# A gated linear-recurrence mixer: its projections as seven block products per pair of matrices, its head outputs through DRAM, its output projection at the end

## The chip, the cores and the metric

The kernel runs on one core of a Trainium2 chip. The metric is the device time of a run in microseconds, as the median of several runs. Engines: TensorE (PE, matmuls, its weight loads as PEld), VectorE (DVE), ScalarE (ACT), GpSimd (POOL) and SyncE (SP, whose queue issues nearly all DMAs). Matmuls write to PSUM banks of 128 partitions by 512 fp32; data otherwise lies in SBUF, 128 partitions wide.

## The reference

One layer on x of 1024 tokens by 1024 channels, in fp32: a mixer, then an MLP, each with RMSNorm ahead and a residual add.

```python
h = rmsnorm(x, norm_mix)
q, f, i, g = split(h @ w_in, 4)              # w_in: 1024 x 4096; 8 heads of 128 channels
log_f = log(lb + (1 - lb) * sigmoid(f));  k = (1 - lb) * sigmoid(-f);  q = silu(q) * 128 ** -0.5
# per head, v = i:  S_t = diag(f_t) S_(t-1) + k_t v_t^T,   o_t = S_t^T q_t
o = o * rsqrt(mean(o * o) + eps) * out_norm * silu(g)        # mean over a head's 128 channels
x = x + o @ w_out
x = x + relu(rmsnorm(x, norm_mlp) @ w1) ** 2 @ w2            # hidden 4096
return rmsnorm(x, norm_final)
```

## The kernel before

Every fp32 product is three matmuls: each operand is split into a rounded part (hi, written by ACT) and the rest (lo, a subtraction on DVE), and split_mm (L171) issues hi·hi, hi·lo, lo·hi.

**Norm and transposes.** x (8 tiles of 128 tokens, xs) is scaled (L144) and turned by PE (L155), so that channels lie on partitions (hT, two halves of 512 tokens, 8 blocks kb of channels).

**Projections, head by head.** proj_qf (L279) makes q and f with channels on partitions: 2 projections × 2 halves × 8 kb × 3 = 96 matmuls of 128x512, tile qf. proj_vg (L323) makes v and g with tokens on partitions: 8 token blocks × 8 kb × 3 = 192 matmuls of 128x256, tile vg. Weights come in pieces of 128x1024 by load_raw (L103) and are split by ensure (L110; L119 on ACT, L120 on DVE), five pieces a head with the one of w_out.

**The scan** of a head is a list of units (scan_units, L350): small, middle, leaf, big(32) and big(64) are small matmuls (tile lv, L366, L399, L417, L447) that fill the decay matrix level by level, each followed by a chain on DVE that carries q, k and f to the next level (carry_q L254, carry_k L261, carry_f L267; prefixes_2 makes qe with two copies on ACT, L388 and L392, and L393 on DVE); kt turns k, kv makes the states S, o_unit the output o, whose squares ACT sums (L499); GpSimd makes the factor rs_z from them (L77 an add, L78 a power), z_unit scales z by it on ACT (L508), and zt turns z (L516). pump (L194) spreads the units over the projections: each three matmuls add 650 (330 for the narrow ones), and when a spacing (2000, or 1800 for the first heads and the last) is reached, the next unit is issued; None is an empty unit. So the program's text fixes PE's order, and every unit must find its chain done. DVE, ACT and POOL take their order from the program up to in_order.close(); behind it a scheduler sets it.

**Output projection.** proj_out (L526): for every head 16 groups of three matmuls of 128x512 (tile op), each added to xs by DVE (L536), one head behind the projections. zt stays in SBUF, split, until then.

**MLP.** It already works by seven block products per pair of blocks (products m1, m2 with banks X, Y, Z; sums of blocks of weights and activations; activations through DRAM, adB and adt). Between mixer and MLP x is normed and turned again (hm and hn, L655).

Of the kernel before, what the change touches and what calls it, by code (L numbers as in the profile page):

```python
# [47 lines left out]
def trunk(ctx: ExitStack, tc: tile.TileContext, x, gains, masks, gfin, w_in, w_out, w1, w2, out):  # L48
# [3 lines left out]
    rstack = ExitStack()  # L52
    res = rstack.enter_context(tc.tile_pool(name="res", bufs=1, side="right", reuse_waits="tile"))
# [49 lines left out]
    def load_raw():  # L103
        i = len(raws)
        if i < len(srcs):
            raw = pool.tile([P, D], F32, name=f"raw{i}", tag="raw", bufs=2)
            nc.sync.dma_start(raw, srcs[i])
            raws.append(raw)

    def ensure(n):  # L110

        while len(split) < min(n, len(srcs)):
            i = len(split)
            raw = raws[i]
            w = pool.tile([P, 2, D], F32R, name=f"w{i}", tag="w", bufs=5)
            step = D // 4 if i < 2 else D
            for c in range(0, D, step):
                o = slice(c, c + step)
                nc.scalar.activation(w[:, 0, o], raw[:, o], AF.Copy)  # L119
                nc.vector.tensor_tensor(w[:, 1, o], raw[:, o], w[:, 0, o].bitcast(F32), ALU.subtract)  # L120
# [897 lines left out]
```

## Time and profile before

| | |
|---|---|
| runs | 1214.08, 1218.25, 1215.22 us; median 1215.22 |
| profiled execution | 1218.23 us, of which the span in the profile 1216.4 us; mean granted clock 0.994 |
| busy in the span | PE 1193.6, DVE 755.9, ACT 516.5, POOL 43.0 us |
| a head in the middle (from one head's first projection to the next head's) | 67.29 us |

The profile shows one execution: a row of the timeline is the start, the duration, the engine, line, operation, output and inputs, shape, and in brackets the idle time ahead with what ended it. A group by line has total busy time, mean ns, and idle time ahead. A row of waits has the total, the count and the longest. Durations of matmuls overlap; their starts don't.

### The profile page before, as it was taken

The page shows a single profiled execution, that of the slowest core. Times are in us where ns is not written, and L with a number is a line of the kernel's source. Part 1 is how long each engine was busy: PE and PEld are TensorE (multiplying, and loading weights), DVE is VectorE, ACT ScalarE, POOL GpSimd, SP SyncE. Part 2 cuts the span into 40 slices and gives each one's busy share as a digit, 9 for nine tenths or more (in the row PEclk, how much of TensorE's full clock was granted, in tenths as well). Part 3 has the DMA queues.
Part 4 walks back from the last instruction along what each step waited for, and adds up shares of the span by engine and source line. Part 5 has one row for each costly group of instructions (what it writes and reads, how often), then busy time and mean ns, then how long its engine had stood idle before and what let it go on. Part 6 is the DMA issues. An engine that isn't in the chain of part 4 may idle for free.

```text
span 1216.4 us, 19005 instructions
## 1 busy us (share of the span) xinstructions
PE 1193.6 (98%) x7980; PEld 1016.7 (84%) x7980; DVE 755.9 (62%) x1071; ACT 516.5 (42%) x899; POOL 43.0 (4%) x78
## 2 busy tenths in 40 slices
PE   8999999999999999999999999999999999999997
PEld 8889889898989899887778888888887888888886
DVE  5475747475665745666865456545657874677663
ACT  6444433333332423335645445454453353233542
POOL 2100000000000000001000000000000000000011
PEclk9999999999999999999999999999999999999999
DMA  6111111111011111113042445224696663522431
GB/s 229 53 54 36 36 53 36 35 37 53 19 53 36 46 44 36 36 36 132 25 173 104 173 173 190 117 109 156 233 339 243 231 215 140 173 70 89 136 121 70
DMA packets 36806, 131.92 MB, mean 108 GB/s; under 512 B 4208, under 2 KB 4336, under 8 KB 36720
## 3 DMA queue, kind: packets, MB, share of 16 engines
q1 hardware_dynamic: 36000, 129.65, 29.8%
q8 instruction: 62, 1.02, 0.3%
q10 hardware_dynamic: 720, 1.07, 0.2%
q14 instruction: 24, 0.20, 0.0%
HBM read 92.95 MB, written 37.75 MB: 107 GB/s over the span
## 4 chain that ended last, share of the span: by engine, by line
PE 90%; DVE 4%; ACT 3%; issue 1%; POOL 1%; DMA 0%; POOLq 0%; DVEq 0%; ACTq 0%
PE vg L172 5%; PE m2X L174 5%; PE m2X L173 5%; PE qf L172 5%; PE m2X L172 5%; PE qf L174 5%; PE qf L173 5%; PE vg L173 5%; PE vg L174 5%; PE m1X L174 4%; PE m1X L172 4%; PE m1X L173 4%; PE m2Y L173 2%; PE m2Y L174 2%; PE m1Y L172 2%; PE m1Y L174 2%
## 5 line engine op out<-in xcount | busy, mean ns | idle before, releaser
L172 PE MATMUL vg<-w,hT 128*128 128x256 f32 x512 | 149.7, 292 | 0.0
L173 PE MATMUL vg<-w,hT 128*128 128x256 f32 x512 | 145.1, 283 | 0.0
L174 PE MATMUL vg<-w,hT 128*128 128x256 f32 x512 | 145.0, 283 | 0.0
L172 PE MATMUL qf<-hT,w 128*128 128x512 f32 x256 | 102.1, 399 | 0.0
L172 PEld LDWEIGHTS vg<-w,hT 128*128 128x128 f32 x512 | 98.2, 192 | 2.8
L174 PE MATMUL qf<-hT,w 128*128 128x512 f32 x256 | 100.2, 391 | 0.0
L173 PE MATMUL qf<-hT,w 128*128 128x512 f32 x256 | 100.0, 391 | 0.0
L173 PEld LDWEIGHTS vg<-w,hT 128*128 128x128 f32 x512 | 98.4, 192 | 0.4
L174 PEld LDWEIGHTS vg<-w,hT 128*128 128x128 f32 x512 | 98.4, 192 | 0.0
L823 ACT ACTIVATE a<-ai 128x1024 fp32r<-128x1024 f32 x56 | 58.9, 1052 | 66.4 <-PE m2X L173 20.5
L536 DVE TENSOR_TENSOR x<-x,op 128x512 f32<-128x512 f32 x120 | 78.3, 684 | 4.6 <-PE op L174 4.3
L824 DVE TENSOR_TENSOR a<-ai,a 128x1024 fp32r<-128x1024 f32 x56 | 68.3, 1220 | 16.2 <-ACT a L823 16.2
L120 DVE TENSOR_TENSOR w<-raw,w 128x1024 fp32r<-128x1024 f32 (+1 forms) x46 | 49.3, 1082 | 16.8 <-ACT w L119 16.6
L174 PEld LDWEIGHTS qf<-hT,w 128*128 128x128 f32 x256 | 48.2, 188 | 10.3
L172 PEld LDWEIGHTS qf<-hT,w 128*128 128x128 f32 x256 | 48.4, 189 | 9.5
L173 PEld LDWEIGHTS qf<-hT,w 128*128 128x128 f32 x256 | 48.3, 189 | 9.3
L172 PE MATMUL op<-w,zt 128*128 128x512 f32 x128 | 52.4, 410 | 1.4 <-DVE x L536 1.4
L706 ACT ACTIVATE e<-e 128x1024 f32<-128x1024 f32 x21 | 22.3, 1062 | 67.6 <-DVE e L858 67.6
L173 PE MATMUL op<-w,zt 128*128 128x512 f32 x128 | 50.6, 395 | 0.0
L174 PE MATMUL op<-w,zt 128*128 128x512 f32 x128 | 50.5, 395 | 0.0
L254 DVE TENSOR_TENSOR q<-q,f 128x512 f32<-128x512 f32 x56 | 38.6, 689 | 16.7 <-PE lv L447 14.5
L119 ACT ACTIVATE w<-raw 128x1024 fp32r<-128x1024 f32 (+1 forms) x46 | 42.8, 944 | 7.9 <-issue 5.1
(667 smaller groups left out, 2947.7 us busy)
## 6 DMA issues: line engine op xcount, KB each, us to landing
raw<-in_w_in SPq DMA_DIRECT2D x32, 512.0 KB, 3.7
ai<-adt SPq DMA_DIRECT2D x32, 512.0 KB, 4.5
adB<-e SPq DMA_DIRECT2D x24, 512.0 KB, 2.6
adt<-t SPq DMA_DIRECT2D x24, 512.0 KB, 4.9
ai<-adB SPq DMA_DIRECT2D x24, 512.0 KB, 4.5
x<-in_x SPq DMA_DIRECT2D x8, 512.0 KB, 7.3
raw<-in_w_out SPq DMA_DIRECT2D x8, 512.0 KB, 4.1
ua<-in_w SPq DMA_DIRECT2D x8, 512.0 KB, 6.0
```

Of the source, the lines that this page charges most:

```text
L119: nc.scalar.activation(w[:, 0, o], raw[:, o], AF.Copy)
L120: nc.vector.tensor_tensor(w[:, 1, o], raw[:, o], w[:, 0, o].bitcast(F32), ALU.subtract)
L172: nc.tensor.matmul(ps, lhi, rhi, start=start, stop=False, **more)
L173: nc.tensor.matmul(ps, lhi, rlo, start=False, stop=False, **more)
L174: nc.tensor.matmul(ps, llo, rhi, start=False, stop=stop, **more)
L254: nc.vector.tensor_tensor(qo, qo, te.to_broadcast([P, n, m]), ALU.mult)
L536: nc.vector.tensor_tensor(xs[tb][:, o], xs[tb][:, o], p_, ALU.add)
L706: nc.scalar.activation(t, t, AF.Relu, scale=sign)
L823: nc.scalar.activation(hi, x, AF.Copy)
L824: nc.vector.tensor_tensor(lo, x, hi.bitcast(F32), ALU.subtract)
```

## The change

q and f are one pair of projections, v and g another, each a product of a 2x2 block matrix (the pair's weights by halves of the input channels) with hn (by halves of channels and of tokens). For heads 1 to 7 each pair is made by seven block products of 4 kb × 3 = 12 matmuls of 128x512 (pair, L405), into three PSUM banks X, Z, Y whose partial results are taken out between the products; head 0's are plain (plain_pair, L379). Everything has channels on partitions, so v needs a unit of its own that turns it (vt, 8 transposes). The sums of blocks: of hn once (values R added by GpSimd, block_sums, split_sum), of weights per pair (four adds and seven splits of 128x512 on DVE, ensure). (1 − lb) of k is folded into q. z is scaled straight from PSUM, multiplied by the gate as it is turned, and stored to DRAM for heads 0 to 6 (z_d). At the mixer's end z and w_out are fetched in halves, split, and the output projection sums over seven heads in PSUM, then head 7, for one half of the columns, and over eight for the other; x, whose tiles were scaled in place, is loaded again (xr). The spacing is 1730. In the MLP some sums are made earlier, and the combinations of block 0 later.

```diff
+SPACING = 1730.0
-FILL = 2
+AHEAD = 6
...
+    def block_sums():
+        for k in range(2):
+            nc.vector.tensor_tensor(R[0, k], R[0, k], R[1, k], ALU.subtract)
+        for k in range(2):
+            nc.vector.tensor_tensor(R[1, k], R[1, 2 + k], R[1, k], ALU.subtract)
+        for k in range(2):
+            nc.vector.scalar_tensor_tensor(R[1, 2 + k], R[0, k], -1.0, R[1, 2 + k], op0=ALU.mult, op1=ALU.subtract)
+        for k in range(2):
+            nc.vector.scalar_tensor_tensor(R[0, 2 + k], R[1, 2 + k], -1.0, R[0, 2 + k], op0=ALU.mult, op1=ALU.subtract)
+    def split_sum(n):
+        half, k0 = SUMS[n]
+        for kb in range(4):
+            r = R[half, k0 + kb // 2][:, kb % 2]
+            if n == "t4":
+                t = hslot(1, kb, f"ht4{kb}")
+            else:
+                t = dslot(("t1", "t2", "t3").index(n) * 4 + kb, [P, 2, 512], f"h{n}{kb}", F32R)
+            hc[n, kb] = t
+            nc.scalar.activation(t[:, 0], r, AF.Copy)
+            nc.vector.tensor_tensor(t[:, 1], r, t[:, 0].bitcast(F32), ALU.subtract)
...
+    PLAIN = 2
+    ORDER = (("X", "a", "B11"), ("Z", "b", "B21"), ("X", "s2", "t2"), ("Y", "s1", "t1"),
+             ("X", "s3", "t3"), ("Y", "s4", "B22"), ("X", "d", "t4"))
...
+    def ensure(count):
+        while len(split) < min(count, len(jobs)):
             i = len(split)
+            n, m = jobs[i]
+            r = raws[n]
+            if m == "s1":
+                add(r["a"], r["a"], r["c"])
+                add(r["c"], r["c"], r["d"])
+            if m == "s2":
+                add(r["c"], r["a"], r["d"])
+            if m == "s4":
+                add(r["c"], r["c"], r["b"])
+            src = r[{"s1": "c", "s2": "c", "s4": "c", "s3": "a"}.get(m, m)]
+            w = mslot(4 + i % 8, [P, 2, 512], f"w{n}{m}", F32R)
+            step = P if i < 1 else 512
+            for c in range(0, 512, step):
                 o = slice(c, c + step)
-                nc.scalar.activation(w[:, 0, o], raw[:, o], AF.Copy)
-                nc.vector.tensor_tensor(w[:, 1, o], raw[:, o], w[:, 0, o].bitcast(F32), ALU.subtract)
+                nc.scalar.activation(w[:, 0, o], src[:, o], AF.Copy)
+                nc.vector.tensor_tensor(w[:, 1, o], src[:, o], w[:, 0, o].bitcast(F32), ALU.subtract)
             split[i] = w
+            if m == "d":
+                load_raw(n + 2)
...
+        def transposes_1(half):
+            def one(kb):
+                flat, g, t = transposed(0, half, kb, xs[4 * half:4 * half + 4])
+                nc.scalar.activation(t[:, 0], flat, AF.Copy, scale=g)
+                nc.vector.scalar_tensor_tensor(t[:, 1], flat, g, t[:, 0].bitcast(F32), op0=ALU.mult, op1=ALU.subtract)
+                if kb % 2 == 0:
+                    R[half, kb // 2] = value(half, kb // 2)
+                nc.gpsimd.tensor_tensor(R[half, kb // 2][:, kb % 2], t[:, 0].bitcast(F32), t[:, 1].bitcast(F32), ALU.add)
+            return [lambda kb=kb: one(kb) for kb in range(KB)]
...
+        def pair(h, tl, j):
+            n = 2 * h + j
+            bank = {}
+            for i, (b, m, src) in enumerate(ORDER):
+                first = b not in bank
+                if first:
+                    bank[b] = psum.tile([P, 512], F32, name=f"p{b}{n}", tag="d")
+                p_ = bank[b]
+                w = weight(n, m)
+                for kb in range(4):
+                    c = slice(kb * P, (kb + 1) * P)
+                    t = hc[src, kb]
+                    split_mm(p_, w[:, 0, c], w[:, 1, c], t[:, 0], t[:, 1], first and kb == 0, kb == 3,
+                             skip_group_check=True)
+                    if kb == 1:
+                        ensure(index[n, m] + AHEAD)
+                    pump(650.0)
+                if m in ("a", "s2", "s4", "b"):
+                    name = "q" if j == 0 else "vT"
+                    tiles(h, tl, name)
+                    half = int(m in ("s2", "s4"))
+                    dst = tl[name][:, HALF[half]]
+                    if m in ("a", "s2"):
+                        nc.scalar.activation(dst, p_, AF.Copy)
+                    else:
+                        add(dst, dst, p_)
+                        if j == 0 and half:
+                            q_part(h, tl, 0, tl["q"])
+                elif m == "s1":
+                    e = part(h, f"e{j}")
+                    nc.scalar.activation(e, p_, AF.Copy)
+                elif m == "s3":
+                    add(e, e, p_)
+                    (f_half, g_half)[j](h, tl, 1, e, -1.0)
+                else:
+                    (f_half, g_half)[j](h, tl, 0, p_, -1.0)
+                    if j == 0:
+                        f_bound(h, tl["f"])
...
+            def vt():
+                v = st["v"] = sp.tile([P, NC, P], F32, name=f"v{h}", tag="v")
+                for g in range(2):
+                    ps = psum.tile([P, 4, P], F32, name=f"vt{h}{g}", tag="s")
+                    for j in range(4):
+                        c = 4 * g + j
+                        nc.tensor.transpose(ps[:, j, :], tl["vT"][:, c * P:(c + 1) * P], ident)
+                    nc.scalar.activation(v[:, 4 * g:4 * g + 4, :], ps, AF.Copy)
+                free("vT")
...
+            def z_unit():
+                for c in range(NC):
+                    nc.scalar.activation(st["z"][:, c, :], st["o"][c // 4][:, c % 4, :], AF.Copy,
+                                         scale=st["r"][:, c:c + 1])
...
+            def zt():
+                z = tl["sg"]
+                for a in range(2):
+                    ps = psum.tile([P, 4, P], F32, name=f"zt{h}{a}", tag="s")
+                    for j in range(4):
+                        nc.tensor.transpose(ps[:, j, :], st["z"][:, 4 * a + j, :], ident)
+                    o = HALF[a]
+                    nc.vector.scalar_tensor_tensor(z[:, o], ps.rearrange("p a b -> p (a b)"), gz[:, h:h + 1], z[:, o],
+                                                   op0=ALU.mult, op1=ALU.mult)
+                    if h < NH - 1:
+                        nc.sync.dma_start(z_d[h][:, o], z[:, o])
+                free("sg")
...
-            return ([None] * (4 if h in (0, NH - 1) else 3) + [small, None, None] + [middle, None, leaf(16, 7)]
-                    + [big(32), big(64), kt, ("values", h), kv, o_unit, z_unit, ("out", h - 2), zt])
+            return ([None] * (6 if h == 0 else 3) + [small, None, None] + [middle, None, leaf(16, 7)]
+                    + [big(32), big(64), None, kt, ("values", h), vt, kv, None, o_unit, z_unit, None, zt])
...
+        heads = {0: {}}
+        tl = heads[0]
+        plain_pair(0, tl, 0, 0)
+        plain_pair(0, tl, 1, 0)
+        while hooks:
+            hook()
+        in_order.close()
+        block_sums()
+        for n in ("t1", "t3", "t2"):
+            split_sum(n)
+        AT = sp.tile([P, NC, P], F32, name="AT", tag="AT")
+        nc.gpsimd.memset(AT, 0.0)
+        plain_pair(0, tl, 0, 1)
+        prefixes(tl)
+        units.extend(scan_units(0, tl))
+        plain_pair(0, tl, 1, 1)
+        split_sum("t4")
+        complete.add(("values", 0))
+        for h in range(1, NH):
+            tl = heads[h] = {}
+            pair(h, tl, 0)
+            prefixes(tl)
+            units.extend(scan_units(h, tl))
+            if h == NH - 1:
+                spacing[0] = LAST_SPACING
+            pair(h, tl, 1)
+            complete.add(("values", h))
...
+        def split_value(t, src):
+            nc.scalar.activation(t[:, 0], src, AF.Copy)
+            nc.vector.tensor_tensor(t[:, 1], src, t[:, 0].bitcast(F32), ALU.subtract)
+        def fetch(what, half, lo, hi):
+            for h0 in range(lo, hi, 2):
+                raw = mslot(item_no[0] % 4, [P, 2, 512], f"i{what}{half}{h0}")
+                item_no[0] += 1
+                for i in range(min(2, hi - h0)):
+                    h = h0 + i
+                    src = z_d[h][:, HALF[half]] if what == "z" else w_out[h * P:(h + 1) * P, HALF[half]]
+                    nc.sync.dma_start(raw[:, i], src)
+                for i in range(min(2, hi - h0)):
+                    h = h0 + i
+                    t = (zh if what == "z" else wo)[half, h] = place(what, half, h)
+                    split_value(t, raw[:, i])
...
+        def proj_out(tbs, dh, hs, after=None):
+            o = HALF[dh]
+            for tb in tbs:
+                c = slice(tb % 4 * P, (tb % 4 + 1) * P)
+                p_ = psum.tile([P, 512], F32, name=f"op{dh}{tb}{hs[0]}", tag="d")
+                for i, h in enumerate(hs):
+                    z, w = zh[tb // 4, h], wo[dh, h]
+                    split_mm(p_, z[:, 0, c], z[:, 1, c], w[:, 0, o0], w[:, 1, o0], i == 0, i == len(hs) - 1)
+                    pump(650.0)
+                add(xs[tb][:, o], xs[tb][:, o], p_)
+                if after:
+                    after(tb)
...
+        fetch("z", 0, 0, last)
+        fetch("w", 0, 0, last)
+        for tb in range(NC):
+            load_x(tb)
+        proj_out(A, 0, range(last))
+        fetch("z", 1, 0, last)
+        fetch("w", 0, last, NH)
+        proj_out(B, 0, range(last))
+        fetch("w", 1, 0, 4)
+        drain_units()
+        for half in range(2):
+            t = zh[half, last] = place("z", half, last)
+            split_value(t, heads[last]["sg"][:, HALF[half]])
+        proj_out(A, 0, (last,))
+        proj_out(B, 0, (last,))
+        fetch("w", 1, 4, NH)
...
-        for _ in range((0, 1, 3, 4)[tb - 4]):
+        for _ in range((0, 2, 3, 3)[tb - 4]):
...
-    combos_1(0, e0)
-    combos_2(0, e0)
...
             prep(k + LOOK)
+            if k == 0:
+                combos_1(0, e0)
+                combos_2(0, e0)
...
         prep(k + LOOK)
+        if m == "a":
+            first_sums(raw2, u, slot(4 + v, [P, D], f"vs3{u}"))
```

Two places in the order. First ACT, the scan of head 7 near the mixer's end (qe7 is made for middle; zh and wo are the split halves of z and w_out, iz and iw what was fetched; the two digits are half and head). Before:

```order
L344 ACTIVATE v7_5253<-vg70_5204 128x256
L345 ACTIVATE sg7_5254<-vg70_5204 128x256
L388 ACTIVATE qe7_5314<-q7_5038 128x32x16
L392 ACTIVATE qe7_5314<-q7_5038 128x32x16
L344 ACTIVATE v7_5253<-vg71_5268 128x256
L345 ACTIVATE sg7_5254<-vg71_5268 128x256
```

The change, same place:

```order
L373 ACTIVATE sig17_4440<-e17_4424 128x512
L687 ACTIVATE zh06_4560<-iz06_4558 128x512
L687 ACTIVATE zh10_4844<-iz10_4841 128x512
L687 ACTIVATE zh11_4847<-iz10_4841 128x512
L687 ACTIVATE wo06_4592<-iw06_4590 128x512
L498 ACTIVATE qe7_4491<-q7_4070 128x32x16
L687 ACTIVATE zh12_4853<-iz12_4850 128x512
L373 ACTIVATE sig07_4520<-pX15_4310 128x512
L502 ACTIVATE qe7_4491<-q7_4070 128x32x16
```

The two copies into qe7 now stand behind four splits of fetched data, where they stood behind evacuations of a projection.

Second DVE, a middle head between middle and big(32), where the carry for distance 16 (q, k, then Ac, then f) is made (lv.._4 and lv.._16 are the matrices of middle and leaf). Before:

```order
L408 COPY_PREDICATED Ac_167<-mk_74,lv3_4_2696 128x16x8
L267 TENSOR_TENSOR f3_2473<-f3_2473 128x64
L346 TENSOR_TENSOR sg3_2567<-sg3_2567,vg32_2675 128x256
L254 TENSOR_TENSOR q3_2406<-q3_2406,f3_2473 128x32x16
L261 TENSOR_TENSOR k3_2472<-k3_2472,f3_2473 128x32x16
L420 COPY_PREDICATED Ac_167<-mk_74,lv3_16_2777 128x256
```

The change:

```order
L518 COPY_PREDICATED Ac_177<-mk_74,lv2_4_1878 128x16x8
L334 TENSOR_TENSOR f2_1553<-f2_1553 128x64
L168 TENSOR_TENSOR w7a_1992<-raw70_1688,w7a_1992 128x512
L147 TENSOR_TENSOR q3_1922<-q3_1922,pZ6_1924 128x512
L168 TENSOR_TENSOR w7b_1995<-raw71_1689,w7b_1995 128x512
L321 TENSOR_TENSOR q2_1385<-q2_1385,f2_1553 128x32x16
L328 TENSOR_TENSOR k2_1552<-k2_1552,f2_1553 128x32x16
L530 COPY_PREDICATED Ac_177<-mk_74,lv2_16_1944 128x256
```

Ahead of the carry stood one product of the gate; now a split of a weight, a sum of the next head's q and another split.

More of the change, by code (lines that the diff above doesn't have):

```diff
@@ L150, in transposes @@
[L150 to L163 removed]
+            nc.vector.tensor_scalar(hn, src, r[:, 0:1], None, op0=ALU.mult)
@@ L208, in trunk @@
     order_all()
+    z_d = [dram.tile([P, T], F32, name=f"zd{h}") for h in range(NH - 1)]
     with tc.tile_pool(name="scan", bufs=1) as sp:
@@ L526, in proj_out @@
-        def proj_out(hs, tbs, after=None):
-            for tb in tbs:
-                c = slice(tb * P, (tb + 1) * P)
-                for dh in range(2):
-                    o = slice(512 * dh, 512 * dh + 512)
-                    p_ = psum.tile([P, 512], F32, name=f"op{hs[0]}{tb}{dh}", tag="d")
-                    for i, h in enumerate(hs):
-                        w, z = weight("a", h, 4), heads[h]["z"]
-                        split_mm(p_, z[:, 0, c], z[:, 1, c], w[:, 0, o], w[:, 1, o], i == 0, i == len(hs) - 1)
-                    nc.vector.tensor_tensor(xs[tb][:, o], xs[tb][:, o], p_, ALU.add)
-                    pump(650.0 * len(hs))
-                if after:
-                    after(tb)
-            if tbs[-1] == NC - 1:
-                complete.update(("out", h) for h in hs)
+                    o = HALF[a]
@@ L560, in trunk @@
             tl = heads[h] = {}
-            if h == 2:
-                spacing[0] = 2000.0
-            for j in range(2):
-                for half in range(2):
-                    proj_qf(h, tl, j, half)
+            pair(h, tl, 0)
             prefixes(tl)
@@ L569, in trunk @@
                 spacing[0] = LAST_SPACING
-            between = None
-            if h == NH - 1:
-                between = lambda b: proj_out((h - 2,), (b,))
-            for half in range(2):
-                proj_vg(h, tl, half, between)
-            complete.add(("values", h))
-            if h < NH - 2:
-                proj_out((h - 1,), range(NC))
-        A, B = range(NC // 2), range(NC // 2, NC)
-        last, prev = NH - 1, NH - 2
-        proj_out((NH - 3,), B)
-        prefetch("a", NH - 3, 4)
@@ L584, in trunk, with place @@
-        proj_out((prev,), range(1))
-        prefetch("a", prev, 4)
-        proj_out((prev,), range(1, FILL))
-        drain_units()
+            pair(h, tl, 1)
+            complete.add(("values", h))
+        zh, wo = {}, {}
+        items = [("z", half, h) for half in (0,) for h in range(NH - 1)] + [("w", 0, h) for h in range(NH)]
+        items += [("z", 1, h) for h in range(NH - 1)] + [("w", 1, h) for h in range(NH)]
+        item_no = [0]
+        def place(what, half, h):
+            if what == "z":
+                return hslot(half, (h, (h + 4) % 8)[half], f"zh{half}{h}")
+            return dslot((h, (8, 9, 10, 11, 0, 1, 2, 3)[h])[half], [P, 2, 512], f"wo{half}{h}", F32R)
@@ L809, in prep @@
     def prep(k):
-        if k >= len(steps):
+        if k >= len(steps) or k in ws:
             return
@@ L818, in prep @@
         if j == 2:
-            hi, lo = (pool.tile([P, 2, 512], F32R, name=f"a{i}{k}", tag="raw", bufs=2) for i in range(2))
+            hi, lo = (mslot(i, [P, 2, 512], f"a{i}{k}", F32R) for i in range(2))
         else:
```

377 lines of the change are left out of this document (164 added, 213 removed).

## The prediction

> **What bounds the kernel now.** I read the page first: busy shares, slices, the chain.
>
> ```profile
> PE 1193.6 (98%) x7980; PEld 1016.7 (84%) x7980; DVE 755.9 (62%) x1071; ACT 516.5 (42%) x899; POOL 43.0 (4%) x78
> PE   8999999999999999999999999999999999999997
> DVE  5475747475665745666865456545657874677663
> PE 90%; DVE 4%; ACT 3%; issue 1%; POOL 1%; DMA 0%; POOLq 0%; DVEq 0%; ACTq 0%
> ```
>
> TensorE (PE) is busy in every slice and holds 90% of the chain that ended last. So time is won by taking matmuls away, and lost wherever PE comes to wait. The price of a matmul is the step between starts, not its 0.39 us, since they are pipelined. From the timeline, a run of 26 steps of the 512-wide kind and one of 47 steps of the 256-wide kind:
>
> ```profile
> 23.03 0.39 PE L172 MATMUL qf<-hT,w 128*128 128x512 f32 x1
> ...
> 28.92 0.39 PE L174 MATMUL qf<-hT,w 128*128 128x512 f32 x1
> 29.15 0.28 PE L172 MATMUL vg<-w,hT 128*128 128x256 f32 x1
> ...
> 34.78 0.28 PE L174 MATMUL vg<-w,hT 128*128 128x256 f32 x1
> ```
>
> (28.92−23.03)/26 = 0.2267 us and (34.78−29.15)/47 = 0.120 us. Next, one steady head in the windows view (columns: PE, PEld, DVE, ACT, POOL busy, clock, DMA share, GB/s):
>
> ```profile
> 174.32:241.61 67.29, 67.29 (x637) 60.20 (x637) 41.44 (x79) 23.87 (x62) 1.91 (x2) 1.00 0.13 40
> ```
>
> In 67.29 us PE never waits, the clock is full, and VectorE (DVE) is busy for 41.44 us, 62%. The PE waits of over 1 us that the view of waits has are these, with the start of the program left out:
>
> ```profile
> PE tr L155 <- DVE hn L144: 4.2, 3, 2.0
> PE tr L655 <- DVE hn L144: 2.9, 2, 2.8
> PE m2Y L172 <- ACT vs12s L624: 1.5, 1, 1.5
> PE op L172 <- DVE x L536: 1.4, 1, 1.4
> PE m1X L172 <- ACT e L846: 1.4, 1, 1.4
> ```
>
> **Matmuls removed and added.** By the order, 768 of 512 columns (qf) and 1536 of 256 (vg) go; 192 (pp) and 1176 (pX, pY, pZ) of 512 come. The 384 of the output projection stay. Removed: 768×0.2267 + 1536×0.120 = 174.1 + 184.3 = 358.4 us; added 1368×0.2267 = 310.1. That is −48.3. The new vt unit turns v by 8 transposes a head:
>
> ```profile
> 287.25 0.93 PE L516 MATMUL zt<-ident,z 128*128 128x128 f32 x7
> ```
>
> 0.93/7 = 0.13, so 64 cost +8.3. Net **−40.0 us**. All of it lies on PE, with nothing to hide it, and is given whole if PE stays fed.
>
> **Waits that may go.** The sums of the second product are made earlier, the combinations of block 0 later, the transposes at the mixer's end are spread otherwise. The m2Y wait (1.5) I count as gone, and half of the other two (2.8): **−2.9**, between 0 and −4.3. The 2.9 us of tr L655 stays: its scaling is where it was.
>
> **DVE in a steady head.** PE's period becomes 67.29 − 96×0.2267 − 192×0.120 + 168×0.2267 + 1.04 = 61.6 with the head's output projection, and 50.7 without its 48×0.2267 = 10.9, which now runs at the mixer's end. What DVE does in it, from groups by line:
>
> ```profile
> L536 DVE TENSOR_TENSOR x<-x,op 128x512 f32<-128x512 f32 x120 | 78.3, 684 | 4.6 <-PE op L174 4.3
> L120 DVE TENSOR_TENSOR w<-raw,w 128x1024 fp32r<-128x1024 f32 (+1 forms) x46 | 49.3, 1082 | 16.8 <-ACT w L119 16.6
> ```
>
> 16 adds of op leave (−10.9), five splits of 1.08 become 14 of about 0.62 (+3.3; half the width, an estimate from 1.08), 8 weight sums come (8×0.68 = +5.4), 6 adds of products (+4.1), and two multiplies of z and two scalings of k go (four at about 0.62, −2.5). 41.4 becomes about 41, now of 50.7: 81%. DVE still isn't the bound, but each chain of the scan has a quarter less time to hide in.
>
> **Where a scan step comes due too early.** Two places, the rows of before:
>
> ```profile
> 277.64 0.61 PE L492 MATMUL o<-v,AT 128*128 128x128 f32 x4
> ...
> 282.42 0.24 POOL L77 TENSOR_SCALAR rs_z<-zs 128x8 f32<-128x8 f32 x1 [65.30 <-ACT z L499]
> ...
> 282.75 1.67 POOL L78 TENSOR_TENSOR rs_z<-rs_z,neghalf 128x8 f32<-128x8 f32 x1
> ...
> 284.45 2.46 ACT L508 ACTIVATE z<-z,rs_z 128x128 f32<-128x128 f32 x8 [2.11 <-POOL rs_z L78]
> ```
>
> z is ready at 286.91, 9.27 us after o began, and its transposes started 9.61 after (287.25): 0.34 to spare. Now o to zt is three spacings of 1730 instead of 2000: 8 steps of three matmuls, 8×0.68 = 5.44, and o's own 3.3 (277.64 to 280.91), so 8.74. PE waits 0.5, and 0.6 more if one DVE operation holds up the short rows on POOL or one copy those on ACT: 1.1.
>
> ```profile
> 179.52 1.31 PE L366 MATMUL lv<-qd,k 128*32 128x80 f32 x64
> ...
> 185.50 0.69 DVE L393 TENSOR_TENSOR qe<-q,f 128x512 f32<-128x512 f32 x1
> ...
> 187.43 0.76 PE L399 MATMUL lv<-qe,k 128*32 128x48 f32 x52
> ```
>
> From small to middle qe needs 6.67 us and had 7.91; now it has 1.3 + 5.44 = 6.7. That leaves nothing, and costs nothing as long as no further DVE operation gets in. At big(32) a split, an add and a split stand ahead of the carry, some 2 us, of which I let 0.35 show. Together 1.5 a head, times 7 (heads 0 to 6): **+10.5**, from 0.3 (+2.1, if DVE's slack absorbs it) to 3.5 (+24.5, if a split lands at each place).
>
> **Head 0.** After the second half's transposes 120 matmuls (27 us) and 8 groups of transposes run until small. In that time DVE has 8 evacuations, 8 block sums and some 23 operations of half that size, about 29 us beside PE's 36. 16 GpSimd adds of 128x512 must be done too; the nearest rows on POOL are these:
>
> ```profile
> 11.53 0.95 POOL L240 MEMSET AT<- 128x1024 f32 x1
> 11.61 1.66 DVE L144 TENSOR_SCALAR hn<-x,rs_n 128x1024 f32<-128x1024 f32 x1 [0.77 <-POOL rs_n L78]
> ```
>
> Two groups of transposes and what follows each (20.52−19.39 = 1.13 us a group):
>
> ```profile
> 19.39 0.60 PE L155 MATMUL tr<-ident,hn 128*128 128x128 f32 x4
> ...
> 20.52 0.60 PE L155 MATMUL tr<-ident,hn 128*128 128x128 f32 x4
> ```
>
> Half a memset is 0.48; a fill reads nothing, so double 0.95 is the other end, and I take 1.2, nearer to a read of two operands. At 1.2 an add about keeps pace with a group's 1.13. **+1**; at 1.9 up to +8, and −2.2 if the second half's waits on hn (two of the three in L155's 4.2) go.
>
> **The mixer's end.** Head 6's z goes to DRAM and back, as others now do early; DMA rows nearest to it:
>
> ```profile
> raw<-in_w_in SPq DMA_DIRECT2D x32, 512.0 KB, 3.7
> ai<-adB SPq DMA_DIRECT2D x24, 512.0 KB, 4.5
> adB<-e SPq DMA_DIRECT2D x24, 512.0 KB, 2.6
> x<-in_x SPq DMA_DIRECT2D x8, 512.0 KB, 7.3
> ```
>
> Store 2.6, read 4.5, the weight behind it on SP 3.7, the two multiplies and splits about 3: 13.8 us after zt. On ACT head 7's qe copies stand behind zh06 and wo06, and DVE's chain behind those copies, another 2 to 3: 16 to 17. Middle is due 60 matmuls and small later, 13.6 + 1.3 = 14.9. So PE waits 1.3 to 2.4, and up to 6 if the reads take the 7.3 that a crowded queue shows. Such a wait also costs clock (windows as above):
>
> ```profile
> 579.00:583.00 4.00, 1.22 (x6) 0.55 (x4) 3.82 (x7) 3.97 (x6) 0.00 (x0) 1.00 0.27 93
> 583.00:587.00 4.00, 3.86 (x17) 3.29 (x18) 2.88 (x5) 2.96 (x5) 0.00 (x0) 0.65 0.00 0
> 587.00:591.00 4.00, 4.00 (x22) 3.28 (x22) 2.00 (x5) 3.04 (x5) 0.00 (x0) 0.92 0.00 0
> ```
>
> After the 2.8 us wait the granted clock is 0.65 and 0.92 for 4 us each: 0.35×4 + 0.08×4 = 1.7 us lost. The Trainium skill (TensorE: Matmul & The Clock Gate, "Part 1: The HAM clock gate") puts the idle window after which the gate closes at about 3.4 us; by it a wait under that would cost no clock, and the term below would be +3.3. The row differs: 2.8 us sufficed, and it decides. I take 3.3 of wait and 1.7 of clock: **+5**, from +1 to +12. Head 7's groups of the projection have only three matmuls (0.68 us), as long as one evacuation on DVE (0.684): **+1**, 0 to 2.
>
> **The sum.** The profiled execution took 1218.2: 1218.2 − 40.0 − 2.9 + 10.5 + 1 + 5 + 1 = 1192.8. It lies 3.0 above the median of 1215.2, so **1190**.
>
> **Rivals.** A, clean: DVE's slack absorbs everything and all waits named go: 1218.2 − 40.0 − 4.3 − 3.0 = 1171. For it speaks that PE waits nowhere in the steady head; against it the 8.74 for 9.27. Chance 0.17.
>
> C, POOL and DVE hold each other up:
>
> ```profile
> L77 POOL TENSOR_SCALAR rs_f<-fs x4: 222/488/936, 1163.2 to 1173.6; 128x1 f32<-128x1 f32 x4
> L78 POOL TENSOR_TENSOR rs_f<-rs_f,neghalf x4: 569/570/1460, 1163.5 to 1174.5; 128x1 f32<-128x1 f32 x4
> ```
>
> The same instruction takes 0.22 or 0.94, 0.57 or 1.46 (the long ones beside DVE operations). With DVE denser both could stretch in each z, 0.71 + 0.89 = 1.6 a head, 11 in seven; the 16 adds in head 0 stretch like the DVE row of 1.66 and cost some 5: 1190 + 16 = 1206. Against it: the eight L78 rows of rs_z before are all 1.67. The Trainium skill (SBUF — State Buffer, "SBUF: two separate sides") calls the port pair of DVE and GpSimd an exclusive lock for a whole instruction when DVE has two SBUF inputs, and the DVE operations added here are mostly such; by it the time would be C's. Chance 0.14.
>
> D, slower: DVE's queue becomes the pace of the scan. Splits and sums of weights, 22 a head, stand in program order among the chains; if three (0.68 each) are ahead of the chain at each of four places (middle, big(32), big(64), the next pair's bank) PE waits 4×2.0 = 8 a head, 56 in seven: 1218.2 − 40.0 − 2.9 + 56 + 7 − 3.0 = 1235. It decides from (40.0 + 2.9 − 7)/7 = 5.1 us a head, seven or eight such operations. Against it: DVE has 19% left and the waits would have to add up, though a wait at one place gives time to the next. Chance 0.09. Between it and the forecast, at 4.6 to 5.6 us a head, lies no change, 0.03. That the matmuls do not go is excluded by the order's count.
>
> **Numbers.** The forecast's own case holds 0.57. About 0.3% (3.6 us) is what a measurement can tell from no change. Faster: 0.57 + 0.17 + 0.14 = 0.88, same 0.03, slower 0.09. The range reaches from A with a little more, 1168, to C with a little more, 1209; D, no change and the ends beyond are left out, under 0.2.
>
> **What would show it.** Right: a steady period near 52 us with PE waits of about 1 us at zt and less at lv L557, DVE near 80% there, and a wait with a lowered clock near the mixer's end. A: no such waits, a period of 50.7. C: L77 and L78 of rs_z above 0.25 and 1.67. D: waits of PE on DVE of 2 us at several units, a period over 56. Wrong altogether: a 512-wide step other than 0.2267 in the block products, or PE waiting for weights from DMA.

## The result and the profile after

The change takes 1184.0 us (median of four runs, 1179.3 to 1186.0) against 1216.7 before in the same comparison: a ratio of 0.973, interval 0.969 to 0.976. The forecast was 1190 with 1168 to 1209. The profiled execution took 1184.61 (span 1182.8), 33.6 less than before's 1218.23; the forecast's sum was −25.4.

The changed kernel's page, the same lines as shown of before:

```profile
PE 1157.9 (98%) x7108; PEld 947.9 (80%) x7108; DVE 797.6 (67%) x1131; ACT 569.8 (48%) x999; POOL 70.7 (6%) x94
PE   8989999999999999999999999999999999999997
DVE  5897868787787867425846545654578756677663
PE 86%; DVE 8%; DMA 2%; POOL 2%; ACT 1%; issue 1%; SPq 0%; POOLq 0%; DVEq 0%; ACTq 0%
```

PE is still busy for 98%, but it holds 86% of the chain instead of 90%: DVE, DMA and POOL now have parts of it. The mixer's slices of DVE went from mostly 4 to 7 tenths to mostly 7 or 8.

Where the time went is clearest by stage. Windows cut at the same events in both kernels: the mixer with the norm behind it, the plain products of the MLP's first block, the rest of its first product, its second product with the end. First before, then after (columns as in the prediction):

```profile
0.00:574.10 574.10, 565.11 (x5237) 503.68 (x5237) 350.31 (x659) 227.95 (x553) 32.86 (x56) 0.99 0.16 56
574.10:626.31 52.21, 49.28 (x227) 40.49 (x225) 37.38 (x50) 31.93 (x49) 0.90 (x2) 0.97 0.21 71
626.31:896.87 270.56, 269.13 (x1178) 220.61 (x1177) 152.38 (x150) 132.92 (x159) 0.00 (x0) 1.00 0.44 167
896.87:1216.40 319.53, 310.02 (x1345) 251.95 (x1343) 215.81 (x214) 123.69 (x140) 9.23 (x20) 0.99 0.45 160
```

```profile
0.00:548.80 548.80, 530.82 (x4364) 435.74 (x4365) 395.51 (x724) 281.99 (x655) 58.98 (x72) 0.98 0.24 79
548.80:596.62 47.82, 47.82 (x227) 39.28 (x226) 36.48 (x46) 31.80 (x48) 0.79 (x2) 1.00 0.23 77
596.62:867.88 271.26, 271.26 (x1177) 220.72 (x1176) 150.07 (x148) 132.07 (x158) 0.00 (x0) 1.00 0.44 166
867.88:1182.80 314.92, 307.98 (x1345) 252.18 (x1343) 215.50 (x214) 123.98 (x140) 10.92 (x20) 0.99 0.46 163
```

The stages changed by −25.3, −4.4, +0.7 and −4.6 us. In the mixer PE was not busy for 9.0 us before (574.1 − 565.1) and is not for 18.0 now: matmuls went, waits came. In the stages behind it, where no matmul went, PE's idle time fell from 13.9 us to 6.9.

The waits of PE on the changed kernel, all of over 1 us but the program's start:

```profile
PE tr L195 <- DVE x L188: 4.7, 4, 1.5
PE lv L509 <- ACT qe L502: 4.4, 1, 4.4
PE lv L509 <- DVE qe L503: 3.1, 1, 3.1
PE kt L572 <- DVE tot L544: 1.9, 1, 1.9
PE lv L557 <- DVE k L328: 1.4, 4, 0.7
```

The first row is at the transposes ahead of head 0's projections, most of it (3.5) at the second half's. Two are single and large at middle (L509): 4.4 for head 7, at the mixer's end, and 3.1 for head 0, while head 1's projections run. The kt is head 0's too. Only the last row belongs to steady heads. There is none at m2Y, m1X, op or tr of hn in the MLP. A steady head, and head 1's projections with head 0's scan beside them:

```profile
130.32:181.37 51.05, 50.95 (x477) 41.88 (x475) 40.34 (x78) 27.56 (x69) 1.92 (x2) 1.00 0.17 52
...
72.51:130.32 57.81, 52.87 (x480) 43.06 (x476) 46.23 (x93) 29.85 (x73) 1.93 (x2) 0.97 0.18 56
```

The steady period is 51.05, against 67.29 with the output projection in it; DVE is busy for 79% of it. Head 1's period is 6.8 us longer.

### The profile page after: what moved, and what is told of

It is laid out like the page before. It is cut to its first block, busy times and chain, and to the rows that moved or that the text cites. A ratio compares the mean times of both kernels' runs of the same rounds, so it can differ in the third digit from the quotient of the medians.

```text
span 1182.8 us, 17554 instructions
## 1 busy us (share of the span) xinstructions
PE 1157.9 (98%) x7108; PEld 947.9 (80%) x7108; DVE 797.6 (67%) x1131; ACT 569.8 (48%) x999; POOL 70.7 (6%) x94
## 4 chain that ended last, share of the span: by engine, by line
PE 86%; DVE 8%; DMA 2%; POOL 2%; ACT 1%; issue 1%; SPq 0%; POOLq 0%; DVEq 0%; ACTq 0%
PE m2X L207 5%; PE m2X L209 5%; PE m2X L208 5%; PE m1X L207 4%; PE m1X L208 4%; PE m1X L209 4%; PE pX L207 3%; PE pX L208 3%; PE pX L209 3%; PE op L207 3%; PE op L208 2%; PE op L209 2%; PE m2Y L207 2%; PE m2Y L209 2%; PE m2Y L208 2%; PE m1Y L207 2%
## 5 line engine op out<-in xcount | busy, mean ns | idle before, releaser
L847 ACT ACTIVATE e<-e 128x1024 f32<-128x1024 f32 x21 | 22.3, 1062 | 67.8 <-DVE e L978 67.8
L207 PE MATMUL op<-wo,zh 128*128 128x512 f32 x128 | 52.4, 409 | 0.0
L208 PE MATMUL op<-wo,zh 128*128 128x512 f32 x128 | 51.2, 400 | 0.0
L209 PE MATMUL op<-wo,zh 128*128 128x512 f32 x128 | 51.2, 400 | 0.0
L147 DVE TENSOR_TENSOR xr<-xr,op 128x512 f32<-128x512 f32 x24 | 16.5, 688 | 46.5 <-PE op L209 46.3
L1005 DVE TENSOR_TENSOR acc<-acc,m2X 128x512 f32<-128x512 f32 x32 | 21.2, 685 | 37.2 <-PE m2X L209 37.1
L328 DVE TENSOR_TENSOR k<-k,f 128x512 f32<-128x512 f32 x56 | 38.4, 686 | 0.1
L844 ACT ACTIVATE e<-e 128x1024 f32<-128x1024 f32 x32 | 34.0, 1062 | 1.0
L534 ACT ACTIVATE AT<-Ac 32x256 f32<-32x256 f32 x32 | 13.3, 415 | 33.7 <-DVE Ac L530 33.4
L147 DVE TENSOR_TENSOR raw<-raw,raw 128x512 f32<-128x512 f32 x42 | 28.9, 689 | 0.7
L209 PEld LDWEIGHTS op<-wo,zh 128*128 128x128 f32 x128 | 24.4, 191 | 6.0
L207 PEld LDWEIGHTS op<-wo,zh 128*128 128x128 f32 x128 | 24.5, 192 | 5.8
L208 PEld LDWEIGHTS op<-wo,zh 128*128 128x128 f32 x128 | 24.5, 191 | 5.5
L300 POOL TENSOR_TENSOR R<-h0B 128x512 f32<-128x512 f32 x16 | 25.5, 1627 | 6.4 <-DVE h0B L297 6.4
L626 ACT ACTIVATE z<-o,rs_z 128x128 f32<-128x128 f32 x64 | 17.4, 384 | 16.4 <-POOL rs_z L122 16.4
L614 PE MATMUL o<-v,AT 128*128 128x128 f32 x128 | 23.4, 275 | 0.0
```

The costliest lines, as they stand in the source:

```text
L147: nc.vector.tensor_tensor(out_, a, b, ALU.add)
L207: nc.tensor.matmul(ps, lhi, rhi, start=start, stop=False, **more)
L208: nc.tensor.matmul(ps, lhi, rlo, start=False, stop=False, **more)
L209: nc.tensor.matmul(ps, llo, rhi, start=False, stop=stop, **more)
L300: nc.gpsimd.tensor_tensor(R[half, kb // 2][:, kb % 2], t[:, 0].bitcast(F32), t[:, 1].bitcast(F32), ALU.add)
L328: nc.vector.tensor_tensor(ke, ke, to.to_broadcast([P, n, m]), ALU.mult)
```

## The experiments

The theory that the runs were to test: PE's matmuls set the time, and the seven products are the gain; part of it is lost where other engines are late for single units, in head 0 and at the mixer's end, and not in the steady heads. The rivals: the gain comes from the output projection's new place and the MLP's order; DVE has become the pace of every head (the prediction's D); GpSimd and DVE hold each other up (its C). Every ratio is to the kernel before, run beside it; a difference in us is that of the ratio to e4_base's, times 1215 (0.1% is 1.2 us). By the intervals of two such ratios, a difference of less than about 3 us can't be told from no change.

**e4_base**, the change again.

> The change itself again, beside the others on the same chip: 0.973 of before, 1184.

1184.4 us, ratio 0.975 (0.973 to 0.977).

**e1_all_plain**, the seven products undone in all heads; the sums of blocks, GpSimd's adds of R among them, go too.

```diff
-    PLAIN = 2
+    PLAIN = 16
...
-            pair(h, tl, 0)
+            plain_pair(h, tl, 0, 0)
+            plain_pair(h, tl, 0, 1)
...
-        block_sums()
-        for n in ("t1", "t3", "t2"):
-            split_sum(n)
```

> Every head's pairs as eight plain block products, as head 0's are; sums of blocks left out since nothing uses them; all else as in the change. Theory (time follows the matmuls; the seven products are where the gain is): 7 heads x 24 x 0.2267 = +38.1 us of matmuls; the waits that the sums cause in head 0 and head 1 (3.5 at the transposes, 3.1 at middle, 1.9 at kt) go, so about +28: 1212, within 0.5% of before. Rival (the gain comes from the output projection at the end and the MLP's order): +10 or less, 1184 to 1194.

1207.9 us, ratio 0.994 (0.992 to 0.996): +22.6, nearer to the theory's 28 than to the rival's 10. Of the 8.5 us of waits that should have gone, 3.3 stayed (1.5 at the second half's transposes, 0.3 at middle, 1.5 at kt), and 1.5 came at big(64). Its first two stages:

```profile
0.00:572.04 572.04, 563.03 (x4533) 465.38 (x4533) 290.16 (x574) 238.09 (x576) 32.05 (x56) 0.99 0.23 76
572.04:619.85 47.81, 47.81 (x227) 39.27 (x226) 36.48 (x46) 31.76 (x48) 0.79 (x2) 1.00 0.24 77
```

The mixer is 23.2 us longer than with the seven products, and PE's idle time in it is back at 9.0. So of 38.1 us of matmuls saved, 23 arrive and 15 are lost again in the mixer: 3.6 by the start of head 1's first projection (72.51 in the change, 68.88 here), 7.1 in the output projection's matmuls (97.3 us from start to start, 90.1 here), and the rest, about 4, in the seven heads between. The other stages are those of the change to 0.1 us: what was won behind the mixer has nothing to do with the products. Without them the mixer is only 2 us shorter than before, and the whole 7 to 8: that much the other edits give, and the rival is out as the main cause.

**e2_mlp_order**, the MLP's order as before.

```diff
-    prep(2)
...
+    combos_1(0, e0)
+    combos_2(0, e0)
...
-        if m == "a":
-            first_sums(raw2, u, slot(4 + v, [P, D], f"vs3{u}"))
...
-        for _ in range((0, 2, 3, 3)[tb - 4]):
+        for _ in range((0, 1, 3, 4)[tb - 4]):
```

> The MLP's order as before (sums of the second product and combinations of block 0 at their old places, hooks 0,1,3,4); the mixer as changed. Theory (these edits took away the waits at m2Y and m1X): +4 to +6 us, PE waits at m2Y of about 2 and at m1X of 1.4 are back. Rival (the 12 us won after the mixer come from the output projection, whose groups of 24 matmuls leave DVE free): +1 or less.

1189.6 us, ratio 0.979 (0.977 to 0.981): +4.7. Two waits are back:

```profile
PE m2Y L207 <- ACT vs12sh L775: 1.5, 1, 1.5
...
PE m1X L207 <- ACT e L969: 1.3, 1, 1.3
```

With the one at L208 that follows them (0.8 in its timeline) and the clock lost they make the 5 us. The stage of the plain products stays at 47.96 us: the wait for hn (2.8) and its clock do not come back with the old order, nor does the wait at op. So the rest of what was won behind the scan is not these edits'. That it is the output projection's is argued, not shown: its groups now have 24 matmuls for one addition on DVE, where they had 6, so DVE is free for the norms.

**e3_sums_on_act**, the values R made by ACT.

```diff
-                nc.gpsimd.tensor_tensor(R[half, kb // 2][:, kb % 2], t[:, 0].bitcast(F32), t[:, 1].bitcast(F32), ALU.add)
+                nc.scalar.activation(R[half, kb // 2][:, kb % 2], flat, AF.Copy, scale=g)
```

> The values R of hn are copied from PSUM by ACT (16 of 128x512) instead of added on GpSimd. Theory P (GpSimd's adds hold up the second half's norms in its queue and stretch DVE's block sums): the PE waits of 3.5 us at the transposes go, DVE's sums take 1.23 each, and middle of head 0 waits under 1.5 instead of 3.1: -5 to -7. Theory D (DVE's own backlog of sums and splits is what middle waits for): the 3.5 at the transposes go, but middle's wait stays over 2.5: -3 to -4.

1195.2 us, ratio 0.984 (0.982 to 0.985): +10.4, where both theories expected a gain. Of PE's waits:

```profile
PE pp L207 <- ACT w1d L167: 4.2, 1, 4.2
PE tr L195 <- DVE x L188: 4.0, 6, 1.2
PE tr L195 <- ACT R L300: 2.3, 2, 1.3
```

ACT, with 16 copies more in the order in which head 0 is written, comes late for everything: the evacuations and the weights. Middle's wait in head 0 fell to 0.3, but middle itself came at 95.9 us instead of 81.0.

**e5_z6_late**, head 6's z taken out of the way of head 7's scan.

```diff
-        fetch("z", 0, 0, last)
-        fetch("w", 0, 0, last)
+        fetch("z", 0, 0, last - 1)
+        fetch("w", 0, 0, last - 1)
...
-        proj_out(A, 0, range(last))
+        proj_out(A, 0, range(last - 1))
...
+        fetch("z", 0, last - 1, last)
+        fetch("z", 1, last - 1, last)
...
-        proj_out(A, 0, (last,))
+        proj_out(A, 0, (last - 1, last))
```

(B likewise.)

> Head 6's z is fetched after the other heads' and joins head 7's groups of the output projection (two heads, six matmuls a group); the first groups sum over six heads. Theory (the round trip of head 6's z through DRAM, ahead of head 7's scan on ACT and DVE, makes the 4.4 to 4.6 us wait at middle, and the clock then lost): the wait falls under 1, -5 to -7 against the change (1177 to 1179). Rival (the scan of head 7 is late anyway, from the density of splits on ACT and DVE there): the wait stays over 3, or comes at the next unit; -2 or less.

1179.6 us, ratio 0.971 (0.968 to 0.973): −5.5, with e11 and e12 the fastest kernel of the study. The wait:

```profile
PE lv L509 <- ACT qe L502: 1.7, 1, 1.7
```

1.7 instead of 4.4 to 4.6, and the granted clock stays at 1.00 in the 8 us behind it. The time is the theory's; the wait did not fall under 1 as it said, and what is left is told by e11.

**e11_z6_late_step**, as e5, with one unit more.

```diff
+                    + [None] * (h == NH - 1)
```

(between small and middle)

> As e5 (head 6's z later), and one empty unit more between small and middle of head 7. Theory (e5's remaining 1.7 us at middle is the chain's lateness alone): the wait falls under 0.3, -1 to -2 against e5, -6 to -7 against the change (1177 to 1178). Rival (the chain on DVE waits for fetched z in order, so that it is late by whatever is fetched): the wait stays over 1, no gain on e5.

1180.4 us, ratio 0.971 (0.969 to 0.973): no gain on e5. Middle's wait fell to 0.5, and 0.6 and 0.9 came at the next two units. Neither bound for the wait was met (under 0.3, over 1), but in time the rival holds: DVE meets the splits of fetched z between the links of head 7's chain, and the lateness only moves.

**e6_values_later**, GpSimd's adds behind the norms.

```diff
-                nc.gpsimd.tensor_tensor(R[half, kb // 2][:, kb % 2], ...)
+                if half:
+                    add_value(half, kb)
...
+        hooks.append(lambda: [add_value(0, kb) for kb in range(KB)])
```

> GpSimd adds the values of hn's first half after the norms of the second half instead of ahead of them in its queue. Theory P (the 3.5 us of PE waits at the second half's transposes come from GpSimd's queue): they fall under 1, -3 to -4 (1180 to 1181); middle's wait in head 0 stays at 3 or grows by up to 1, since the sums come no earlier. Rival (the waits come from DVE or ACT at that place): they stay over 2.5, -1 or less.

1187.5 us, ratio 0.977 (0.975 to 0.979): +2.1, which can't be told from no change, where −3 to −4 was expected. The waits at the second half's transposes stayed at 3.5 us. Middle's in head 0 fell to 1.5, and 3.4 came at a weight of head 0's (w1d). The norms' factors were ready early now, but look at the scaling of x on DVE, twice two of them, and at GpSimd:

```profile
26.34 1.41 DVE L188 TENSOR_SCALAR x<-x,rs_n 128x1024 f32<-128x1024 f32 x2
...
28.27 3.43 DVE L188 TENSOR_SCALAR x<-x,rs_n 128x1024 f32<-128x1024 f32 x2
```

```profile
28.15 25.48 POOL L297 TENSOR_TENSOR R<-h0B 128x512 f32<-128x512 f32 x16
```

Two scalings take 1.41, and 3.43 as soon as GpSimd adds beside them. Theory P, the queue, was only half of it: the adds hold DVE up wherever they stand.

**e9_t4_on_pool**, four subtractions moved from DVE to GpSimd.

```diff
-            nc.vector.tensor_tensor(t[:, 1], r, t[:, 0].bitcast(F32), ALU.subtract)
+            (nc.gpsimd if on_pool else nc.vector).tensor_tensor(t[:, 1], r, t[:, 0].bitcast(F32), ALU.subtract)
...
-        split_sum("t4")
+        split_sum("t4", True)
```

> GpSimd instead of DVE makes the lo parts of the last block sum of hn (t4, 4 of 128x512), which stand on DVE ahead of head 0's small chain (2.5 us there). Theory D (DVE's amount of work is what head 0's chains wait for): middle's wait falls from 3.1 to about 1, -2 to -3 with the clock (1181 to 1182). Theory C (GpSimd with two operands in SBUF stretches the DVE operations beside it): DVE's rows at that place lengthen by 2 us or more, middle's wait stays over 2.5, 0 to -1.

1186.3 us, ratio 0.975 (0.973 to 0.977): no difference. DVE's work became less, and middle's wait in head 0 grew from 3.1 to 6.0 (kt's fell from 1.9 to 0.6). DVE beside GpSimd and after it, then GpSimd:

```profile
74.56 1.78 DVE L168 TENSOR_TENSOR w2d<-raw,w2d 128x512 fp32r<-128x512 f32 x1
76.26 1.77 DVE L147 TENSOR_TENSOR raw<-raw,raw 128x512 f32<-128x512 f32 x1
...
78.74 0.68 DVE L168 TENSOR_TENSOR w2s<-raw,w2s 128x512 fp32r<-128x512 f32 x1
```

```profile
71.10 6.38 POOL L112 TENSOR_TENSOR ht<-R,ht 128x512 fp32r<-128x512 f32 x4 [7.10 <-ACT ht L111]
```

The same operation takes 0.68 alone and 1.78 beside GpSimd. That is C's mechanism, at full size. The Trainium skill (SBUF — State Buffer, "SBUF: two separate sides") says that the two share a port pair under an exclusive lock for whole instructions, when DVE has two inputs in SBUF or runs in a mode that uses two ports; these rows, with two inputs in SBUF, agree. A four-operation help of 2.5 us lengthened DVE's rows beside it by 3.5 in all.

**e12_sums_on_dve**, e5 with the values R on DVE, none on GpSimd.

```diff
-                nc.gpsimd.tensor_tensor(R[half, kb // 2][:, kb % 2], ...)
+                nc.vector.tensor_tensor(R[half, kb // 2][:, kb % 2], ...)
```

> As e5 (head 6's z later), and the 16 adds of the values R on DVE instead of GpSimd, so that GpSimd touches no operand of 512 in head 0. If DVE's amount of work decides (theory D): 16 x 0.6 = 9.6 us more on DVE, of which it had about 5 free ahead of small: middle's wait grows from 3.1 by 3 to 5, +2 to +5 against e5 (1182 to 1185). If GpSimd's adds cost as much as they take off DVE (theory C: DVE stretched by 3 us there, and the second half's norms held up in GpSimd's queue by 3.5): the waits at the transposes go, middle's wait grows by 3 at most, 0 to -4 against e5 (1176 to 1180).

1179.7 us, ratio 0.970 (0.969 to 0.972): as e5. Its waits in head 0:

```profile
PE pp L209 <- DVE w1d L168: 3.9, 1, 3.9
PE pp L208 <- DVE h0B L297: 2.0, 4, 0.7
...
PE tr L195 <- DVE x L188: 1.8, 2, 1.2
```

Those at the second half's transposes and at middle (0.4 now) went, and others came, for a weight of head 0's that stands behind the adds. The 16 adds cost the same time either way. But the stretching alone does not take back what GpSimd takes off DVE: from 14 to 72 us DVE is busy for 55.1 us here and for 48.3 in e5. How much of the cost on GpSimd is stretching and how much its queue, no run separates.

**e7_head0_later**, two empty units more ahead of head 0's scan.

```diff
-            return ([None] * (6 if h == 0 else 3) + [small, None, None] + [middle, None, leaf(16, 7)]
+            return ([None] * (8 if h == 0 else 3) + [small, None, None] + [middle, None, leaf(16, 7)]
```

> Head 0's scan starts two empty units (3.6 us) later: 8 instead of 6. Theory D (DVE's backlog of block sums and splits at that place delays head 0's chains by 3 us): the 3.1 at middle and the 1.9 at kt fall under 0.7 each; with the clock -4 to -6 (1178 to 1180). Rival (the density of DVE in head 1's first pair holds the chains up wherever they stand): half of the waits stay, -2 or less.

1187.8 us, ratio 0.978 (0.976 to 0.980): +3.5. Theory D, which expected −4 to −6, fell in this form: middle still waits for 2.9, 3.4 us later, because DVE filled the time with the next pair's splits and sums, which are ready, and took up the chain at 79.1 instead of 75.4. The scan of head 7 came later as well, and its wait was 5.7.

**e8_dve_plus8**, 56 operations on DVE that nothing uses.

```diff
+                        if m in ('a', 's2', 's3', 's4'):
+                            nc.vector.tensor_tensor(dum, dum, dum, ALU.mult)
```

> Eight more DVE operations of about 0.6 us per head (multiplications of 128x432 that nothing uses), put with the weights' splits and sums. Theory (DVE's slack, 10 us of 51 in a head, takes them): +1 to +6 in all, DVE near 90%. Rival (the prediction's D: operations ahead of a chain come out as waits of PE, one for one): 7 heads x 4.8 = +25 or more.

1194.1 us, ratio 0.982 (0.980 to 0.984): +8.3, between the two and nearer to the theory. They did not spread as meant: nothing holds them back, and the order put all 56 ahead of 211 us. So one reads single heads. A head with 22 of them (13.3 us), the next with five (3.0 us), and a later one with none:

```profile
132.88:187.41 54.53, 52.47 (x476) 43.06 (x475) 50.28 (x101) 27.47 (x69) 2.47 (x2) 0.97 0.16 49
187.41:241.98 54.57, 52.50 (x476) 42.99 (x475) 45.02 (x91) 28.23 (x70) 1.91 (x2) 0.97 0.16 52
```

```profile
241.98:293.36 51.38, 51.05 (x476) 41.92 (x475) 40.48 (x78) 27.72 (x69) 1.91 (x2) 1.00 0.17 52
```

In the first DVE has 10 us more to do, 92% of the period. Both periods are 3.5 us longer, by a wait of 2.1 at middle, whose chain stands behind added operations, and by the clock: 0.58 and 0.59 in the 4 us behind the waits, 1.7 us lost each time. Together the two heads have 16.3 us of added operations and are 7.0 longer. So more than half of the work came out of DVE's slack, which is real, and D's one for one is out; but at middle operations ahead of a chain do come out as a wait of PE, as D says.

**e10_spacing_1500**, units closer together.

```diff
-SPACING = 1730.0
+SPACING = 1500.0
```

> Spacing 1500 instead of 1730: o to zt and small to middle are 7 steps of three matmuls each instead of 8. Theory (the chains fit 1730 with 0.1 to 0.3 us to spare, as their rows say, so that the next step costs): waits of 0.6 to 0.8 us at zt and 0.4 to 0.5 at middle in each of heads 1 to 6, +6 to +10 (1190 to 1194). Rival (a unit that waits gives the next ones time, and DVE catches up): +2 or less.

1196.0 us, ratio 0.984 (0.981 to 0.986): +10.4, just above what was expected, and at other places than said:

```profile
PE lv L476 <- DVE qd L458: 5.8, 4, 1.6
...
PE pX L207 <- DVE e L147: 4.8, 5, 2.3
PE lv L509 <- DVE qe L503: 4.7, 2, 3.6
PE lv L509 <- ACT qe L502: 2.4, 5, 0.8
```

Middle's 0.4 a head came as expected; at zt there was no wait that the view lists, and small and the seventh product's bank wait instead. That the scan has next to no time to spare at 1730 is shown, its weakest places were not those of the prediction.

## Why the prediction was right, and where it was wrong

**The matmuls.** Right. The steps are as taken (a steady period of 51.05 where 50.7 was worked out without waits). vt cost 0.10 us a transpose instead of 0.13 (6.3 instead of 8.3): −42.0 instead of −40.0. The prediction had divided the 0.93 us that a row of seven lasts, its last matmul's full duration included, where its own rule says to go by starts.

**Waits that may go.** Mis-sized, and the largest error: −2.9 forecast, −12.9 measured. The last three stages give −8.3. Another 3.6 are at the transposes of hm, which lie in the mixer's window and took 6.9 us from start to start, now 3.2. And 1.0 is at head 7's zt, whose eight transposes came 0.29 apart before, each waiting for its block of z, and now 0.10. The step that failed is "The 2.9 us of tr L655 stays: its scaling is where it was". The scaling, before and now:

```profile
581.68 1.41 DVE L144 TENSOR_SCALAR hn<-x,rs_n 128x1024 f32<-128x1024 f32 x2
```

```profile
553.35 1.41 DVE L188 TENSOR_SCALAR hn<-xr,rs_n 128x1024 f32<-128x1024 f32 x2
```

It began 7.6 us behind the first plain product (574.10) and begins 4.6 behind it now (548.80). Its place in the program was the same, but what DVE and ACT had to do ahead of it was not; which of the edits did this stays open (e2 says only that the MLP's order did not). With that wait went the 1.7 us of clock that the prediction itself had read from the rows behind it. The m2Y and m1X waits went because of the MLP's order (e2).

**The steady head.** DVE at 40.3 of 51.05, 79%, where 41 and 81% were forecast: right. The stalls: 1.5 a head forecast, and heads 2 to 7 have together 5.1 us (their periods less 50.45 each, which is 50.7 with vt at its measured cost), 0.9 a head. PE is idle for only 0.1 to 0.7 of it; the rest lies in the products' steps, which around the units are longer than 0.2267 (pX's average 0.240). Middle (nothing) and big(32) (0.2 to 0.7 for 0.35) were right. The 1.1 at zt failed:

```profile
159.06 0.60 PE L614 MATMUL o<-v,AT 128*128 128x128 f32 x4
...
165.88 2.18 ACT L626 ACTIVATE z<-o,rs_z 128x128 f32<-128x128 f32 x8 [2.13 <-POOL rs_z L122]
...
167.96 1.03 PE L635 MATMUL zt<-ident,z 128*128 128x128 f32 x8
```

zt began 8.90 after o, and the last of eight copies of z ended at 168.06, behind its start: a transpose needs only its own block of z, and the blocks come one by one. The chain is 9.0 long, near the 9.27 read before; what it is compared with was the wrong end of zt.

**Head 0.** Mis-sized: +1 forecast, about 3.5 measured. This is a remainder: −25.3 + 42.0 + 3.6 + 1.0 = 21.3 are lost in the mixer, less 12.5 in the heads' periods and 5.3 at the end; against e1 the change is 3.6 late when head 1's projections start. Head 1's period has 7.4 more, with head 0's chains in it: 3.1 at middle, 1.9 at kt, and 1.7 of clock, of which this row has most:

```profile
81.30:85.30 4.00, 3.99 (x72) 3.27 (x73) 4.00 (x11) 0.63 (x1) 0.00 (x0) 0.64 0.59 145
```

The sum of the heads' stalls, 5.1 + 7.4 = 12.5, is near the 10.5 forecast, but more than half of it lies in one head and at other units, so that is luck and no success. C's mechanism, which the prediction had priced at 5 us for head 0, is at work: GpSimd's adds took 1.28 to 2.32 us (1.2 was taken), and DVE was stretched beside them (e6, e9). DVE's amount of work there has its part too, and no run gives the shares. C's other half, the short rows of rs_z, did not occur: they took 0.24 and 1.67 as before. What no run could buy back is the amount itself: on GpSimd, on DVE or on ACT the 16 adds cost PE about the same or more (e5 and e12, e3).

**The mixer's end.** Right in place, and near in size: +6 forecast with the short groups, 5.3 measured (the output projection's matmuls took 97.3 us from start to start instead of 91.9). The parts were off both ways. The wait was longer, 4.4 instead of 1.3 to 2.4, within its bound of 6. Against e1, which has the same groups without that wait, wait and clock cost 7.1 where 5 were taken; so the groups themselves cost nothing against before. The rows, ACT, then DVE, SP and PE:

```profile
437.75 0.63 ACT L687 ACTIVATE zh<-iz 128x512 fp32r<-128x512 f32 x1 [3.62 <-DMA iz<-zd]
...
442.29 0.61 ACT L498 ACTIVATE qe<-q 128x512 f32<-128x512 f32 x1
```

```profile
438.41 0.69 DVE L688 TENSOR_TENSOR zh<-iz,zh 128x512 fp32r<-128x512 f32 x1 [3.43 <-ACT zh L687]
439.02 0.30 DVE L487 COPY_PREDICATED Ac<-mk,lv 128x128 f32<-128x128 uint8 x1
```

```profile
427.47 0.86 SPq L640 DMA_DIRECT2D zd<-sg  x2
...
433.58 0.32 SPq L698 DMA_DIRECT2D iz<-zd  x1
```

```profile
445.51 1.51 PE L509 MATMUL lv<-qe,k 128*32 128x48 f32 x64 [4.38 <-ACT qe L502]
```

The store of z was issued at 427.5, its reading only at 433.6, and its split on ACT came at 437.8, as the prediction's chain has it. It had seen ACT's copies behind that split; DVE's subtraction of the same z stands ahead of the whole small chain too, so both waited. The granted clock behind the wait:

```profile
441.00:447.00 6.00, 1.61 (x66) 1.37 (x65) 6.00 (x14) 3.00 (x7) 0.00 (x0) 0.77 0.92 309
447.00:451.00 4.00, 4.00 (x13) 3.14 (x11) 3.02 (x9) 2.37 (x4) 0.00 (x0) 0.50 0.39 136
```

0.50 for 4 us is about 2 us, as forecast (1.7).

The sum as measured: −42.0 − 12.9 + 12.5 + 3.5 + 5.3 = −33.6, head 0's term being what the others leave. The time came out 8.2 us lower than the sum's −25.4 because 10 us more of waits went than forecast and the matmuls and the end gave 2.7 more, against 4.5 that the heads' stalls and head 0 cost beyond their terms.

## What to carry to other kernels

A product that block sums save is worth its matmuls only where the additions that it costs lie under other work: here 23 of 38 us arrived, and 10.7 of the 15 lost were at the two ends of the stage, where work has no neighbour to hide under, not in its steady part. Before one counts a wait as staying because its instruction has not moved, one looks at what else its engine loses at that place. A chain that goes through DRAM and back should not stand in order, on any engine, ahead of a chain that the bottleneck waits for: taking one such head out of the way gave 5.5 us, and the kernel at 0.971 of before is faster than both.

## What the runs showed of the hardware

GpSimd is no free helper for DVE. An addition of 128x512 on GpSimd took 1.28 us alone and up to 2.32 beside DVE; DVE's operations of 0.68 took up to 1.78 beside it, and two scalings of 128x1024 3.43 instead of 1.41, though those have a single tensor operand. In head 0 a GpSimd operation of one column took 0.77 us beside such scalings and 0.22 otherwise. Those of 8 columns took 0.24 or 0.25 and 1.67 or 1.68 in all eight heads, but that is hardly a test: beside most of them DVE was idle or read an operand from PSUM. Only in head 6 did a DVE operation with two operands in SBUF run beside the 1.67, and it took its usual 0.69.

A long wait of PE cost more than itself. Behind idle times of 1.7 us (middle of head 7 in e5) and 1.9 (kt of head 0) the granted clock stayed at 1.00; behind 2.1 (e8), 2.8 (before) and 3.1 (middle of head 0) it fell to 0.58 to 0.65 over 4 us, which is 1.4 to 1.7 us more. Several short ones did the same: behind the waits of 0.9, 1.5 and 1.2 at the second half's transposes, within 5 us, it was 0.50 from 34 to 38 us.
